# A hybrid encoder layer on one core: the dense products in seven block products instead of eight

## The chip, the cores and the metric

The kernel runs on one core of one Trainium2 chip. The core has a matrix engine (TensorE, PE in the profile; its weight loads are PEld), a vector engine (VectorE, DVE), an activation engine (ScalarE, ACT), a general engine (GpSimd, POOL) and a queue engine that starts DMA transfers (SyncE, SP). The metric is the device time of one execution in microseconds (us), and lower is better.

## The reference, cut to what matters

One layer is computed for 1024 prompt tokens and 32 sample tokens, 1056 in all, with D_MODEL = 1024 and D_FF = 2816, in float32.

```python
def swiglu(x, w_gate, w_up, w_down):
    return (jax.nn.silu(x @ w_gate) * (x @ w_up)) @ w_down

x = x + 0.5 * rmsnorm(swiglu(rmsnorm(x, ffn1_norm_pre), ffn1_w_gate, ffn1_w_up, ffn1_w_down), ffn1_norm_post)
h = rmsnorm(x, mix_norm_pre)
a, b, q, k, v, g = split(h @ w_in)                 # six blocks of 512 columns
u = a * sigmoid(b)
c = silu(layernorm(depthwise_conv31(concat(conv_hist, u))))
r = silu(g) * groupnorm(retention(rope(q), rope(k), v, R0)) * ret_gn_g   # 4 heads of 128
x = x + rmsnorm(concat([c, r]) @ w_out, mix_norm_post)
x = x + 0.5 * rmsnorm(swiglu(rmsnorm(x, ffn2_norm_pre), ffn2_w_gate, ffn2_w_up, ffn2_w_down), ffn2_norm_post)
```

The results are the new x of all tokens, the last 30 rows of u and the retention states.

## The kernel before, in words

Everything is held transposed: 128 channels on the partitions, tokens along the free dimension. The 1056 tokens are cut into three chunks `CH` of 416, 384 and 256 columns. A weight matrix is used in blocks of 128 x 128, 1312 of them in the whole layer. To keep float32 accuracy each operand is split into a high part (rounded to the matrix engine's fp32r format by an ACT copy) and a low part (the difference, a subtraction), and each product is three matmuls: high x high, high x low, low x high. That is `gemm`, lines 155 to 157.

`weight` loads 128 x 1024 weights into `raw`, writes `whi` on ACT (line 137) and `wlo` on GpSimd (line 138). `split_x` makes `xh` and `xl` of the tokens, with the norm's gain but without the norm's factor; that factor, `rbc`, is multiplied onto the result later, so the products need not wait for it.

`ffn` goes through eight groups of two or three blocks of 128 FFN channels. In each it makes gate and up products for the three chunks (`glu_unit`, tiles `pg` and `pu`; DVE lines 309, 313 and 317, ACT lines 311 and 316), splits the gated value in SBUF, and multiplies it at once by the down weights, so that gated values never leave the chip. The down products `pd` are added to `y` in SBUF by DVE (line 335). `mixer` makes the GLU and the convolution's 31 taps (DVE, lines 413 and 416, over all tokens at once, 1086 columns), the heads' q, k, v and g, and the retention in pieces of up to 128 tokens (`retain`). Between mixer and `out_proj` the results stay in SBUF too. Norms (`norm`, `pre_norm`, `post_norm`) sum squares (ACT line 229, DVE line 233), turn them into a factor and spread it over the partitions by a matmul.

The order of the work is set by two things. Small pieces that follow a product are put on a list (`later`) and emitted after a given stretch of matrix time. The framework's scheduler then places each instruction in its engine's queue, and each engine runs its queue in that order. DMAs are all started by SP.

Of the kernel before, what the change touches and what calls it, by code (L numbers as in the profile page):

```python
# [10 lines left out]
F32 = mybir.dt.float32  # L11
F32R = mybir.dt.float32r
# [7 lines left out]
NF = FF // P  # L20
TS = 32
# [3 lines left out]
CH = [(0, 416), (416, 384), (800, 256)]  # L25
RCH = [[(0, TS), (32, P), (160, P), (288, P)], [(0, P), (128, P), (256, P)], [(0, P), (128, P)]]
GAP = 30
LCH = [(0, 446), (446, 384), (830, 256)]
LGR = [[(0, P), (128, P), (256, P), (384, 62)], RCH[1], RCH[2]]
# [4 lines left out]
GAMMA = [1.0 - 2.0 ** (-5 - h) for h in range(H)]  # L34

# [8 lines left out]
# Depths of the rotating buffers, and delays between dependent pieces of work in us of TensorE time.  # L44
TMP_BUFS = 4
SS_BUFS = 4
RET_BUFS = 2
TBUFS = {"t": TMP_BUFS, "ss": SS_BUFS, "sq": 2, "sg": 2, "dg": 1}
TAP_STEP = 0.9
RET_DELAY = (4.0, 10.0, 5.0, 3.5)  # L50
NORM_DELAY = (3.0, 2.5)
TILE_DELAY = 0.004
DOWN_DELAY = 4.0
DOWN_DELAY_END = 3.0
RET_DELAY_LAST = (2.5, 5.0, 2.0, 3.0)
CNORM_STEP = 11.0
CNORM_DELAY = (46.0, 5.0, 7.0, 5.0)
OUT_UNITS = 2
GROUPS = [[0, 1], [2, 3, 4], [5, 6, 7], [8, 9, 10], [11, 12, 13], [14, 15, 16], [17, 18, 19], [20, 21]]
# [3 lines left out]
def layer_kernel(ctx: ExitStack, tc: tile.TileContext, a: dict, o: dict):  # L63
# [4 lines left out]
    wsp = ctx.enter_context(tc.tile_pool(name="wsp", bufs=6))  # L68
    raw = ctx.enter_context(tc.tile_pool(name="raw", bufs=2))
    yp = ctx.enter_context(tc.tile_pool(name="yp", bufs=1))  # L70
    act = ctx.enter_context(tc.tile_pool(name="act", bufs=17))
    tmp = ctx.enter_context(tc.tile_pool(name="tmp", bufs=2))
    sml = ctx.enter_context(tc.tile_pool(name="sml", bufs=2))
    psm = ctx.enter_context(tc.tile_pool(name="psm", bufs=4, space=PS))
# [5 lines left out]
    idh = cst.tile([P, P], F32, name="idh")  # L80
    one = cst.tile([P, P], F32, name="one")
    mhalf = cst.tile([P, 4], F32, name="mhalf")
    on512 = cst.tile([P, P], F32, name="on512")
    rcol = [cst.tile([P, 4], F32, name=f"rcol{c}") for c in range(len(CH))]
    rsq = [cst.tile([P, 4], F32, name=f"rsq{c}") for c in range(len(CH))]
    rbc = [cst.tile([P, n], F32, name=f"rbc{c}") for c, (_, n) in enumerate(CH)]
# [7 lines left out]
    # Work that follows a matrix product is emitted a given stretch of TensorE time later, between other products.  # L94
# [11 lines left out]

    def step():
        t, _, fn = heapq.heappop(pend)
        now[0] = max(now[0], t)
        fn()  # L110
# [5 lines left out]
    ready = [False] * len(CH)  # L116
    waiting = [[] for _ in CH]

    def scaled(c, fn):
        if ready[c]:  # L120
            fn()
        else:
            waiting[c].append(fn)

# [3 lines left out]
    def weight(src, eng=None, pieces=1):  # L128
        r = raw.tile([P, KD, P], F32, name=nm("raw"), tag="raw")
        hi = wsp.tile([P, KD, P], F32R, name=nm("whi"), tag="wh")  # L130
        lo = wsp.tile([P, KD, P], F32R, name=nm("wlo"), tag="wl")
        s, m = src.rearrange("p (k c) -> p k c", k=KD), KD // pieces

        def piece(i):
            e = slice(i * m, (i + 1) * m)
            nc.sync.dma_start(out=r[:, e], in_=s[:, e])
            nc.scalar.activation(hi[:, e], r[:, e], AF.Copy)  # L137
            (eng or nc.gpsimd).tensor_tensor(lo[:, e], r[:, e], hi[:, e], ALU.subtract)  # L138

        if pieces > 1:  # L140
            return (hi, lo), piece
        piece(0)
        return hi, lo

    def xtile(c, dt, s):
        return act.tile([P, CH[c][1]], dt, name=nm(s), tag=f"x{c}")

    def ttile(n, s, tag="t"):
        return tmp.tile([P, LCH[0][1]], F32, name=nm(s), tag=tag, bufs=TBUFS[tag])[:, :n]

    def gemm(ps, wx, start=True, stop=True):
        last = len(wx) - 1
        n = ps.shape[1]
        for i, ((wh, wl), (xh, xl)) in enumerate(wx):
            nc.tensor.matmul(ps, wh, xh, start=start and i == 0, stop=False)  # L155
            nc.tensor.matmul(ps, wh, xl, start=False, stop=False)  # L156
            nc.tensor.matmul(ps, wl, xh, start=False, stop=stop and i == last)  # L157
            advance(3 * (n / 2400 + 0.0025))

    def ytile(c, k, s):  # L160
        return yp.tile([P, CH[c][1]], F32, name=nm(s), tag=f"y{c}_{k}")

    def proj(c, w, xn, s):
        while len(xn[c]) < KD or None in xn[c]:
            step()
        p = mmt(CH[c][1], s)
        gemm(p, [((w[0][:, k], w[1][:, k]), xn[c][k]) for k in range(KD)])
        return p

    def mmt(n, s):  # L170
        return psm.tile([P, 512], F32, name=nm(s), tag="mm")[:, :n]

    def stt(n, s, tag="st"):
        return pss.tile([P, 512], F32, name=nm(s), tag=tag)[:, :n]

    def norm(ss, n, groups, inv, ident, done, rpre=None, rout=None, dt=(1.0, 2.5)):
        def first():
            m = len(groups)
            sp = stt(4, "sp")
# [530 lines left out]
```

## Time and profile before

| | |
|---|---|
| median of 3 runs | 2104.08 us (2102.23 to 2105.53) |
| span of the profiled execution | 2102.2 us |
| busy: PE, PEld | 2017.4 us (96%), 1980.6 us (94%) |
| busy: DVE, ACT, POOL | 995.9 us (47%), 535.9 us (25%), 641.9 us (31%) |
| matmuls recorded | 12384 |
| DMA | 124.65 MB, 59 GB/s in the mean |

The page gives the span of the profiled execution, which is its own time as far as it is known; the three timed runs lie between the span and 3.3 us above it. Rows of instruction groups read: line, engine, operation, output and inputs by the program's names, shapes and count, then the time busy, the mean of one in ns, and the engine's idle time just before them with what ended it. Rows of a stretch read: start and end, its length, then busy time and number of instructions for PE, PEld, DVE, ACT and POOL, the granted clock of the matrix engine, the busy share of the DMA engines, and GB/s. Rows in order of time read: start, duration, engine, line, operation.

### The profile page before, as it was taken

To read this page: it belongs to the slowest core of one execution; us is meant where nothing else is said; L and a number is where in the kernel's file an instruction comes from. 1 tells how busy PE (TensorE), PEld (TensorE's weight loads), DVE (VectorE), ACT (ScalarE), POOL (GpSimd) and SP (SyncE) were. 2 spreads that over 40 slices of the span, in tenths; PEclk is the share of its full clock that TensorE was granted. 3 is DMA by queue.
4 is the path that set the end of the run, shared out by engine and by line. 5 is a ranking of instruction groups with operands and counts; after the bars stand their busy time and mean duration, and the time that the engine had idled before them with its cause. 6 is when DMAs were issued, how large, how long until landed. Compare 5 with 4: busy or idle time off the path is not lost. (4 is left out here: it accounts for less than half of the span.)

```text
span 2102.2 us, 29594 instructions
## 1 busy us (share of the span) xinstructions
PE 2017.4 (96%) x12384; PEld 1980.6 (94%) x12384; DVE 995.9 (47%) x1623; ACT 535.9 (25%) x987; POOL 641.9 (31%) x386
## 2 busy tenths in 40 slices
PE   8999999999999998988989998999999999999996
PEld 7999999999999997887888997899999999999996
DVE  7123232323232378899998629513232323232336
ACT  6321212121202144223324635331111111111121
POOL 2212212121212135456546427411212121212114
PEclk9999999999999999999999999899999999999998
DMA  5111111111111232111101135211111111111113
GB/s 178 60 41 51 41 51 41 51 41 51 41 51 43 70 113 88 60 41 43 35 16 46 57 105 166 87 41 41 51 41 51 41 51 41 51 41 51 41 39 126
DMA packets 54133, 124.65 MB, mean 59 GB/s; under 512 B 7536, under 2 KB 31728, under 8 KB 54000
## 3 DMA queue, kind: packets, MB, share of 16 engines
q1 hardware_dynamic: 54000, 122.76, 17.8%
q8 instruction: 97, 1.59, 0.3%
q14 instruction: 36, 0.29, 0.0%
HBM read 109.12 MB, written 13.62 MB: 58 GB/s over the span
## 5 line engine op out<-in xcount | busy, mean ns | idle before, releaser
L138 POOL TENSOR_TENSOR wlo<-raw,whi 128x1024 fp32r<-128x1024 f32 (+1 forms) x171 | 421.4, 2469 | 1146.2 <-ACT whi L137 1142.5
L156 PE MATMUL pg<-xl,whi 128*128 128x256 f32 (+2 forms) x1152 | 375.5, 326 | 10.6 <-DVE xl L240 10.5
L155 PE MATMUL pg<-xh,whi 128*128 128x256 f32 (+2 forms) x1152 | 378.3, 329 | 7.2 <-ACT xh L239 6.4
L157 PE MATMUL pg<-xh,wlo 128*128 128x256 f32 (+2 forms) x1152 | 374.4, 325 | 0.7 <-DVE wlo L138 0.7
L155 PE MATMUL pd<-hh,whi 128*128 128x256 f32 (+2 forms) x1056 | 341.9, 325 | 5.2 <-DVE y L335 5.0
L156 PE MATMUL pu<-xl,whi 128*128 128x256 f32 (+2 forms) x1056 | 343.9, 326 | 0.0
L155 PE MATMUL pu<-xh,whi 128*128 128x256 f32 (+2 forms) x1056 | 343.5, 325 | 0.0
L157 PE MATMUL pu<-xh,wlo 128*128 128x256 f32 (+2 forms) x1056 | 342.4, 324 | 0.0
L156 PE MATMUL pd<-hl,whi 128*128 128x256 f32 (+2 forms) x1056 | 342.3, 324 | 0.0
L157 PE MATMUL pd<-hh,wlo 128*128 128x256 f32 (+2 forms) x1056 | 341.2, 323 | 0.0
L137 ACT ACTIVATE whi<-raw 128x1024 fp32r<-128x1024 f32 (+1 forms) x174 | 180.7, 1047 | 589.2 <-PE pd L156 391.6
L335 DVE TENSOR_TENSOR y<-y,pd 128x416 f32<-128x416 f32 (+2 forms) x336 | 172.7, 519 | 238.9 <-PE pd L157 238.6
L313 DVE TENSOR_TENSOR h<-sg,pu 128x416 f32<-128x416 f32 (+2 forms) x132 | 68.7, 521 | 397.2 <-PE pu L157 396.2
L156 PEld LDWEIGHTS pg<-xl,whi 128*128 128x128 f32 x1152 | 218.8, 190 | 13.4 <-DVE xl L240 12.2
L155 PEld LDWEIGHTS pg<-xh,whi 128*128 128x128 f32 x1152 | 219.1, 190 | 9.3 <-ACT xh L239 6.4
L157 PEld LDWEIGHTS pg<-xh,wlo 128*128 128x128 f32 x1152 | 219.2, 190 | 1.5 <-DVE wlo L138 0.9
L155 PEld LDWEIGHTS pd<-hh,whi 128*128 128x128 f32 x1056 | 200.8, 190 | 6.9 <-DVE y L335 5.6
L157 PEld LDWEIGHTS pd<-hh,wlo 128*128 128x128 f32 x1056 | 201.2, 191 | 1.0
L155 PEld LDWEIGHTS pu<-xh,whi 128*128 128x128 f32 x1056 | 200.6, 190 | 1.1
L156 PEld LDWEIGHTS pd<-hl,whi 128*128 128x128 f32 x1056 | 201.1, 190 | 0.5
L157 PEld LDWEIGHTS pu<-xh,wlo 128*128 128x128 f32 x1056 | 200.7, 190 | 0.8
L156 PEld LDWEIGHTS pu<-xl,whi 128*128 128x128 f32 x1056 | 200.7, 190 | 0.4
(154 smaller groups left out, 2683.8 us busy)
## 6 DMA issues: line engine op xcount, KB each, us to landing
raw<-in_wgu SPq DMA_DIRECT2D x86, 512.0 KB, 3.5
raw<-in_wd SPq DMA_DIRECT2D x44, 512.0 KB, 3.5
raw<-in_wo SPq DMA_DIRECT2D x16, 512.0 KB, 3.4
x<-x SPq DMA_DIRECT2D x32, 208.0 KB, 3.1
x<-x SPq DMA_DIRECT2D x32, 192.0 KB, 2.7
x<-x SPq DMA_DIRECT2D x32, 128.0 KB, 2.1
x<-in_x SPq DMA_DIRECT2D x16, 208.0 KB, 4.1
x<-in_x SPq DMA_DIRECT2D x16, 192.0 KB, 4.0
```

The source lines that it names most:

```text
L137: nc.scalar.activation(hi[:, e], r[:, e], AF.Copy)
L138: (eng or nc.gpsimd).tensor_tensor(lo[:, e], r[:, e], hi[:, e], ALU.subtract)
L155: nc.tensor.matmul(ps, wh, xh, start=start and i == 0, stop=False)
L156: nc.tensor.matmul(ps, wh, xl, start=False, stop=False)
L157: nc.tensor.matmul(ps, wl, xh, start=False, stop=stop and i == last)
L313: nc.vector.tensor_tensor(h32, sg, pu, ALU.mult)
L335: nc.vector.tensor_tensor(ys[c][k], ys[c][k], pd, ALU.add)
```

## The change

All dense products (gate, up, down, w_in, w_out) are done by the scheme of Strassen in Winograd's form. Two blocks of input channels, two blocks of output columns and two quarters of 264 tokens make a 2 x 2 product of blocks; it takes seven block products of sums instead of eight of blocks. The tokens are now two halves j of 528 columns, each two quarters of Q = 264.

- Weights: the host hands over the four blocks of each 2 x 2 apart. `prep` loads them into four `raw` tiles, makes four sums on DVE (lines 158, 159, 164, 167) and splits all seven into `whi` (ACT, line 151) and `wlo` (GpSimd, or DVE for two of them, line 152). Its steps run between the products of the visit before.
- Tokens: `tbuild` makes the seven token operands of a pair of channel blocks: four sums of 264 columns, two high parts on ACT, two low parts (three together as `tal`, four together as `tbl`).
- Products: `visit` runs seven products of `nk` pairs of channel blocks into three PSUM tiles `px` (two buffers), `pz` and `py` (one each). Several products go into the same bank one after the other, and each bank is read in between: eight reads, four of them copies on ACT (line 211) and four additions on DVE (line 214), or eight additions on DVE where the result is summed over blocks (line 209).
- The norm's factor is applied to the tokens before the splits (`pre_norm`), so the products wait for the norm.
- The gated values go to DRAM (`hd`); the down products run after all gate and up products, in four blocks `DBLK` of 3, 3, 3 and 2 pairs, each of which loads `hd` through two buffers (`gtile`) and builds its token operands.
- The convolution's taps run by halves, the convolution's and the heads' outputs go through DRAM (`cd`, `rd`), retention takes five pieces in each half instead of nine in all, and the rotary products move wholly to GpSimd.
- `load` and `held` tie a DMA's place in the order to the last matmul emitted.

```diff
+    def prep(src, nk, dve_lo=()):
+            a11, a21, a22, a12 = (wp.tile([P, 4 * P], F32, name=nm("raw"), tag="raw", bufs=5)[:, :nk * P] for _ in range(4))
...
+            def split(x):
+                nc.scalar.activation(hi, x, AF.Copy)
+                (nc.vector if len(ws) in dve_lo else nc.gpsimd).tensor_tensor(lo, x, hi, ALU.subtract)
...
+            split(a11)
+            nc.vector.tensor_tensor(s1, a21, a22, ALU.add)
+            nc.vector.tensor_tensor(a21, a11, a21, ALU.subtract)
+            split(s1)
+            split(a12)
+            nc.vector.tensor_tensor(a11, s1, a11, ALU.subtract)
+            split(a11)
+            nc.vector.tensor_tensor(a12, a12, a11, ALU.subtract)
+            split(a12)
+            split(a22)
+            split(a21)
...
+    def tbuild(f, dst, j, kp, pool_lo=False):
+        v.tensor_tensor(f[:, 1], f[:, 7], f[:, 0], ALU.subtract)
+        nc.scalar.activation(tah, f[:, 0:3], AF.Copy)
+        v.tensor_tensor(tal, f[:, 0:3], tah, ALU.subtract)
+        v.tensor_tensor(f[:, 3], f[:, 4], f[:, 1], ALU.subtract)
+        v.tensor_tensor(f[:, 6], f[:, 4], f[:, 7], ALU.subtract)
+        v.tensor_tensor(f[:, 5], f[:, 2], f[:, 3], ALU.subtract)
+        nc.scalar.activation(tbh, f[:, 3:7], AF.Copy)
+        (nc.gpsimd if pool_lo else v).tensor_tensor(tbl, f[:, 3:7], tbh, ALU.subtract)
...
+    def visit(ws, tj, nk, dst, acc, after, between):
+        x = bank("px", 2)
+        product(0, x, True)
+        first(dst[0], x)
+        z = bank("pz", 1)
+        product(1, z, True)
+        first(dst[3], z)
+        y = bank("py", 1)
+        product(2, y, True)
+        add(dst[0], y)
+        product(3, x, False)
+        first(dst[1], x)
+        product(4, z, False)
+        add(dst[1], z)
+        y = bank("py", 1)
+        product(5, y, True)
+        first(dst[2], y)
+        product(6, x, False)
+        add(dst[3], x)
+        add(dst[2], x)
...
+            def build(j, ht=ht, k0=k0, nk=nk):
+                for k in range(nk):
+                    f = gtile("hf")
+                    for i, to in enumerate(pieces(f)):
+                        load(to, two(hd[2 * (k0 + k) + i, :, half(j)]))
+                    tbuild(f, ht, j, k, k % 2 == 1)
```

A unit of weights serves both halves (two visits) or, at the edges of a stage where the halves come one after the other, one half (one visit); in the second case the weights are loaded and prepared again for the other half.

Where it moves instructions, three places. First, VectorE in the down products, before: the end of a group's gated values (tg, h, hl) and then nothing but the additions of products to y.

```order
L309 TENSOR_TENSOR tg_3209<-pg_3159,rbc_97 128x384
L313 TENSOR_TENSOR h_525_3213<-sg_3211,pu_3184 128x384
L317 TENSOR_TENSOR hl_3216<-h_525_3213,hh_3215 128x384
L309 TENSOR_TENSOR tg_3269<-pg_3219,rbc_98 128x256
L313 TENSOR_TENSOR h_532_3273<-sg_3271,pu_3244 128x256
L317 TENSOR_TENSOR hl_3276<-h_532_3273,hh_3275 128x256
L335 TENSOR_TENSOR y_778<-y_778,pd_3297 128x416
L335 TENSOR_TENSOR y_787<-y_787,pd_3308 128x416
```

After, in the second down block: additions from the banks (ys from px, pz, py) stand between the sums of the next token operands (hf), their low parts and the weight sums (raw, s).

```order
L209 TENSOR_TENSOR ys_5731<-ys_5731,py_6732 128x264
L214 TENSOR_TENSOR ys_5731<-ys_5731,px_6679 128x264 x2
L186 TENSOR_TENSOR hf_6664<-hf_6664 128x264
L189 TENSOR_TENSOR hf_6664<-hf_6664 128x264
L190 TENSOR_TENSOR hf_6664<-hf_6664 128x264
L191 TENSOR_TENSOR hf_6664<-hf_6664 128x264
L188 TENSOR_TENSOR tal_6668<-hf_6664,tah_6667 128x792
L193 TENSOR_TENSOR tbl_6670<-hf_6664,tbh_6669 128x1056
L209 TENSOR_TENSOR ys_5733<-ys_5733,px_6754 128x264
L209 TENSOR_TENSOR ys_5733<-ys_5733,pz_6777 128x264
L214 TENSOR_TENSOR ys_5733<-ys_5733,py_6795 128x264
L164 TENSOR_TENSOR raw_6764<-s_936_6787,raw_6764 128x384
```

Additions on which a single PSUM bank waits now have token and weight sums ahead of them on the same engine. Second, VectorE in the mixer, before: taps (cv) of one column block alternate with reads of products (q, k, g).

```order
L413 TENSOR_SCALAR cv_7867<-u_6928,vec 128x1086
L416 SCALAR_TENSOR_TENSOR cv_7867<-u_6928,vec,cv_7867 128x1086
L573 TENSOR_TENSOR q_8059<-pq_8030,cos_6912 128x416
L416 SCALAR_TENSOR_TENSOR cv_7867<-u_6928,vec,cv_7867 128x1086 x2
L573 TENSOR_TENSOR k_8095<-pk_8066,cos_6912 128x416
L416 SCALAR_TENSOR_TENSOR cv_7867<-u_6928,vec,cv_7867 128x1086 x5
L579 TENSOR_TENSOR g_8162<-pg_8133,rbc_96 128x416
```

After, early in the mixer: a tap of half the length (cu), then token sums of the second half (xf), a weight sum (raw), a weight's low part (wlo) and reads of products (cu from py, pz, px).

```order
L214 TENSOR_TENSOR cu_9947<-cu_9947,py_9998 128x264
L158 TENSOR_TENSOR s_1592_9990<-raw_9963,raw_9964 128x512
L485 SCALAR_TENSOR_TENSOR cu_9328<-cu_9328,vec 128x558
L189 TENSOR_TENSOR xf_9588<-xf_9588 128x264
L189 TENSOR_TENSOR xf_9603<-xf_9603 128x264
L188 TENSOR_TENSOR tal_9592<-xf_9588,tah_9591 128x792
L214 TENSOR_TENSOR cu_9947<-cu_9947,pz_9975 128x264
L188 TENSOR_TENSOR tal_9607<-xf_9603,tah_9606 128x792
L159 TENSOR_TENSOR raw_9963<-raw_9962,raw_9963 128x512
L214 TENSOR_TENSOR cu_9947<-cu_9947,px_9948 128x264
L152 TENSOR_TENSOR wlo_9994<-s_1592_9990,whi_9993 128x512
L485 SCALAR_TENSOR_TENSOR cu_9328<-cu_9328,vec 128x558
```

The taps keep their number of elements and stand among work that was not there. Third, the queue of SP at the start, before: weights first, then half of the last chunk of x.

```order
L612 DMA vec<-in_vec 128x196
L136 DMA raw_105<-in_wgu 128x512
L136 DMA raw_108<-in_wgu 128x512
L260 DMA x_117<-in_x 128x256
L260 DMA x_119<-in_x 128x256
```

After: both halves of x, then the first weights.

```order
L704 DMA vec<-in_vec 128x196
L712 DMA x_88<-in_x 128x528 x4
L712 DMA x_93<-in_x 128x528 x4
L715 DMA idn<-in_idn 128x128
L716 DMA msk<-in_msk 128x128
L712 DMA x_123<-in_x 128x528 x4
L712 DMA x_128<-in_x 128x528 x4
L146 DMA raw_160<-in_wgu 128x512
```

Sixteen transfers of x now stand ahead of the first weights.

More of the change, by code (lines that the diff above doesn't have):

```diff
@@ new lines, in layer_kernel, with unit, run @@
+    program = []
+    def unit(src, nk, visits, dve_lo=()):
+        program.append((src, nk, visits, dve_lo))
+    def run():
+        made = [prep(s, nk, dl) for s, nk, _, dl in program]
+        for _ in made[0][1]:
+            pass
+        for n, (src, nk, visits, _) in enumerate(program):
+            ws = made[n][0]
+            nxt = made[n + 1][1] if n + 1 < len(program) else iter(())
+            for i, (before, tj, dst, acc, after) in enumerate(visits):
+                if before:
+                    before()
+                last = i == len(visits) - 1
+                visit(ws, tj, nk, dst(), acc, after, (lambda: next(nxt, None)) if last else lambda: None)
+            made[n] = None
@@ new lines, in post_norm, with done @@
+    def post_norm(j, ys, ss, res, g, mul, out, gpre, dst):
+        def done(rb):
+            s2 = None
+            for q in range(2):
+                xs = gtile("xs")
+                for k in range(4):
+                    load(flat(xs[:, 2 * k:2 * k + 2]), res[4 * q + k, :, half(j)])
+                for k in range(4):
+                    y = ys[4 * q + k]
+                    nc.vector.scalar_tensor_tensor(y, y, col(g, 4 * q + k), rb, ALU.mult, ALU.mult)
+                    (nc.vector if gpre is None and k % 2 else nc.gpsimd).tensor_tensor(y, y, xs[:, 2 * k:2 * k + 2], ALU.add)
+                    nc.sync.dma_start(out=out[4 * q + k, :, half(j)], in_=flat(y))
+                    if gpre is not None:
+                        s2 = square(s2, y)
+            if gpre is not None:
+                pre_norm(j, ys, s2, gpre, dst)
+        norm(ss, 1.0 / D, mul, done)
@@ new lines, in layer_kernel, with then @@
+    hu(1, (0, 1))
+    cu(2, (0, 1))
+    cu(3, (0, 1))
+    for j in (0, 1):
+        hu(2, (j,), True)
+        hu(3, (j,), True)
+        src, nk, vs, dl = program[-1]
+        b, tj, dst, acc, after = vs[0]
+        def then(after=after, j=j):
+            after()
+            free(j)
+        program[-1] = (src, nk, [(b, tj, dst, acc, then)], dl)
+    out_proj(xt[2], x1, "mpost", x2, "f2pre", xt[3])
+    ffn(xt[3], a["wgu2"], a["wd2"], x2, "f2post", o["y"], None, None, 2)
+    run()
+    flush()
```

848 lines of the change are left out of this document (397 added, 451 removed).

## The prediction

> **What bounds the kernel now.** I read the page's busy shares first, then busy time by stage, then the start times of consecutive matmuls, then pairs of VectorE and GpSimd instructions that run at the same time, and last the groups by form for prices.
>
> ```profile
> span 2102.2 us, 29594 instructions
> PE 2017.4 (96%) x12384; PEld 1980.6 (94%) x12384; DVE 995.9 (47%) x1623; ACT 535.9 (25%) x987; POOL 641.9 (31%) x386
> ```
>
> TensorE is the bound over the whole; no other engine is half busy. The average hides one stage. The next rows are stretches of the span (us from its start), with busy time of PE, PEld, DVE, ACT and POOL: first the FFN, then the mixer, then the output product, then the second FFN.
>
> ```profile
> 65.00:784.00 719.00, 716.93 (x4432) 713.27 (x4431) 234.87 (x374) 141.63 (x228) 153.15 (x69) 1.00 0.16 52
> 784.00:1184.00 400.00, 357.62 (x2195) 336.95 (x2194) 368.95 (x584) 139.74 (x308) 223.00 (x167) 0.97 0.15 48
> 1184.00:1284.00 100.00, 99.39 (x624) 98.03 (x623) 44.30 (x77) 42.87 (x82) 43.55 (x27) 1.00 0.36 116
> 1290.00:2060.00 770.00, 757.95 (x4638) 751.26 (x4637) 269.05 (x440) 160.18 (x269) 179.68 (x91) 0.99 0.16 53
> ```
>
> In the FFNs PE never stops and DVE has two thirds of its time free. In the mixer DVE is busy 369 of 400 us, more than PE. So a cheaper matmul pays in the FFNs and hardly in the mixer, and added VectorE work costs at once in the mixer.
>
> **What a matmul costs.** These are starts of matmuls in a full stretch; between them lie 36 matmuls of 416 columns, 48 of 384 and 48 of 256.
>
> ```profile
> 299.82 0.35 PE L155 MATMUL pg<-xh,whi 128*128 128x416 f32 x1
> 306.62 0.34 PE L155 MATMUL pg<-xh,whi 128*128 128x384 f32 x1
> 315.07 0.28 PE L155 MATMUL pg<-xh,whi 128*128 128x256 f32 x1
> 320.82 0.35 PE L155 MATMUL pg<-xh,whi 128*128 128x416 f32 x1
> ```
>
> Start to start is 0.1889, 0.1760 and 0.1198 us. Before, each of 3936 weight passes (1312 blocks by three) runs over the three chunks: 3936 x 0.4847 = 1908 us of the 2102. After, the order holds 13,776 matmuls of 264 columns. Eight columns above 256, at the slope between 256 and 384 (0.00044 us a column), give 0.1233 us, so 1699 us: TensorE's products lose 209 us, 11%, not an eighth, because the narrower matmul pays its fixed part more often. [...]
>
> **What VectorE and GpSimd cost each other.** Here are four instructions of the FFN (DVE, POOL, DVE, POOL) and six of the mixer.
>
> ```profile
> 322.35 2.42 DVE L317 TENSOR_TENSOR hl<-h,hh 128x256 fp32r<-128x256 f32 x1 [0.83 <-ACT hh L316]
> 322.09 2.40 POOL L138 TENSOR_TENSOR wlo<-raw,whi 128x1024 fp32r<-128x1024 f32 x1 [0.48 <-ACT whi L137]
> 344.36 0.42 DVE L313 TENSOR_TENSOR h<-sg,pu 128x256 f32<-128x256 f32 x1 [2.52 <-PE pu L157]
> 342.48 2.40 POOL L138 TENSOR_TENSOR wlo<-raw,whi 128x1024 fp32r<-128x1024 f32 x1 [17.99 <-ACT whi L137]
> ...
> 1002.34 0.15 DVE L501 SCALAR_TENSOR_TENSOR nb<-mv,rs 128x1 f32<-128x1 f32 x1
> ...
> 1012.75 1.34 DVE L416 SCALAR_TENSOR_TENSOR cv<-u,vec,cv 128x1086 f32<-128x1086 f32 x1
> 1014.00 0.55 DVE L573 TENSOR_TENSOR q<-pq,cos 128x384 f32<-128x384 f32 x1
> 1014.47 1.64 DVE L416 SCALAR_TENSOR_TENSOR cv<-u,vec,cv 128x1086 f32<-128x1086 f32 x1
> 1013.27 1.69 POOL L574 TENSOR_TENSOR sw<-sw,sin 128x384 f32<-128x384 f32 x1 [2.15 <-ACT sw L572]
> 1015.04 1.96 POOL L575 TENSOR_TENSOR q<-q,sw 128x384 f32<-128x384 f32 x1
> ```
>
> The 256-column subtraction of two SBUF tensors took 2.42 us and ended 0.28 us after the GpSimd instruction beside it; 256 columns at 0.96 a ns are 0.27 us. It stood still until GpSimd was through. The product that reads PSUM took 0.42 us in the same situation. In the mixer taps and GpSimd take turns: the tap at 1012.75 ends at 14.09, GpSimd's product ends at 14.96, the next tap at 16.11, GpSimd's sum at 17.00. [...]
>
> **Prices.**
>
> ```profile
> L138 POOL TENSOR_TENSOR wlo<-raw,whi 128x1024 fp32r<-128x1024 f32 (+1 forms) x171 | 421.4, 2469 | 1146.2 <-ACT whi L137 1142.5
> L335 DVE TENSOR_TENSOR y<-y,pd 128x416 f32<-128x416 f32 (+2 forms) x336 | 172.7, 519 | 238.9 <-PE pd L157 238.6
> L335 DVE TENSOR_TENSOR y<-y,pd 128x256 f32<-128x256 f32 x112 | 46.5, 420 | 63.8 <-PE pd L157 63.8
> L317 DVE TENSOR_TENSOR hl<-h,hh 128x416 fp32r<-128x416 f32 x44 | 26.1, 592 | 25.5 <-ACT hh L316 25.3
> L138 DVE TENSOR_TENSOR wlo<-raw,whi 128x1024 fp32r<-128x1024 f32 x1 | 1.2, 1221 | 0.0
> L416 DVE SCALAR_TENSOR_TENSOR cv<-u,vec,cv 128x1086 f32<-128x1086 f32 x120 | 193.2, 1610 | 0.9
> L501 DVE SCALAR_TENSOR_TENSOR nb<-mv,rs 128x1 f32<-128x1 f32 x28 | 29.5, 1055 | 4.6 <-POOL rs L498 4.6
> L138 POOL TENSOR_TENSOR wlo<-raw,whi 128x512 fp32r<-128x512 f32 x2 | 2.6, 1316 | 7.3 <-ACT whi L137 7.3
> L442 POOL TENSOR_TENSOR sin<-sin,rbc 128x256 f32<-128x256 f32 x1 | 0.7, 735 | 0.0
> L137 ACT ACTIVATE whi<-raw 128x1024 fp32r<-128x1024 f32 x170 | 178.3, 1057 | 586.5 <-PE pd L156 391.6 <-PE pg L156 65.5 <-issue 54.5
> L333 ACT ACTIVATE y<-pd 128x256 f32<-128x256 f32 x16 | 6.1, 382 | 4.5 <-PE pd L157 4.5
> ```
>
> DVE: 0.157 us plus columns/960 (592 at 416, 1221 at 1024). Queued instructions start some 0.08 us before the one ahead has ended (the tap at 1012.75 ends at 1014.09, its successor starts at 1014.00), so I count 0.08 less each. GpSimd: 0.735 at 256 and 2.40 at 1024 give 0.18 us plus 2.17 ns a column: 1.01 at 384, 1.29 at 512, 2.47 at 1056.
>
> **The change, part by part.** *PSUM evictions.* Each visit of a pair of weight columns by a token half reads its banks eight times. 928 adds on DVE at 0.35 us are 325 us, for 336 adds of 173 us before; the other 544 copies go to ACT at 0.39 (382 at 256), 212 us. *Weight sums.* 472 new DVE additions (0.61, 0.48 and 0.34 us at 512, 384 and 256 columns), 258 us. *Low halves of weights.* Seven where four were: GpSimd 474 x 1.29 + 168 x 1.01 + 80 x 0.74 = 840 us against 421 before; 104 more on DVE, 55 us. *Token sums (tbuild).* 408 DVE instructions, 207 us, in place of the splits of x and h; 48 large ones on GpSimd, 119 us. *Taps.* 248 half-length ones, 159 us alone, where 120 take 161 us alone (1.34 each). *Gated values, norms, squares:* 290 instructions of 528 columns, 183 us. Retention (40 chunks for 36), diagonals and small pieces: 90 us. DVE sums to 1270 us, GpSimd (with rotary, residual sums and GLU) to 1130 where it was busy 642. ACT comes to about 1050 us, nowhere above two thirds of a stage, so I cost it at nothing. DRAM: the gated values are stored and read again, some 56 MB more on 123; the queues stood at 52 GB/s in the FFN rows above and have carried 327 at the start (row below), so only latency counts.
>
> By stage, from the order of the new kernel. **Gate and up** (each FFN): TensorE 3696 x 0.1233 = 456 us, DVE 172 to 194, GpSimd some 230. TensorE stays the bound; 911 us for both, where they took 352 blocks x 3 x 0.4847 = 512 each. Gain 113. **Down**: TensorE 1848 x 0.1233 = 228 us. DVE 219 us in FFN 1 and 199 in FFN 2, GpSimd about 150, now in the same stretch. How much of GpSimd's time does DVE lose? Above nothing, at most all. The mixer before is the nearest: taps lost 120 x (1.61 - 1.34) = 32 us, the one-column nb 28 x (1.055 - 0.15) = 25, smaller groups about 24 by the same subtraction: 81 us, against some 177 that GpSimd's work there needs alone, 0.46. So DVE takes 219 + 69 = 288 and 268 us, 560 for both (256 each before, TensorE's price). Cost 48. **Mixer and output product**: DVE 355 + 96 = 451 us, GpSimd 340, so 451 + 0.46 x 340 = 607; DVE was 92% busy in the mixer before, I take 95% and 640 us, where it took 500. Cost 140. TensorE has 331 us of products there and some 80 of retention and norms (357.6 less 192 x 3 x 0.4847 before). What hid such work before, TensorE's own time, is gone there.
>
> **Edges.**
>
> ```profile
> 7.00:20.00 13.00, 11.12 (x60) 9.63 (x59) 12.19 (x23) 12.57 (x28) 5.56 (x3) 1.00 0.95 327
> 6.40 0.58 PE L155 MATMUL pg<-xh,whi 128*128 128x256 f32 x1 [6.40 <-ACT xh L239]
> 2088.45 0.42 DVE L233 TENSOR_TENSOR ss<-ss,sq 128x256 f32<-128x256 f32 x1 [0.21 <-ACT sq L229]
> x<-x SPq DMA_DIRECT2D x32, 208.0 KB, 3.1
> ```
>
> *Start.* TensorE began at 6.4 us because the norm's factor was applied after the product. Now all of x (4.3 MB, 14 us at 327 GB/s) is queued ahead of the first weights, the norm must be done before the first token sum, and its PSUM copies stand on ACT behind 16 squares and 7 weight splits: first product near 28 us, a stream near 40, so 35 us are lost. *Each of eight down blocks* loads its hd tiles through two buffers; the third tile waits for a build and a 3.1 us load: 2.5 us each beyond DVE's sum, 20 us. *FFN 2's first single visits* run beside the norm of the second half: 15 us. *Tail*: from the last square (2088.5) to the end were 14 us; with 528 columns 20.
>
> Sum: 35 + 911 + 560 + 640 + 20 + 15 + 20 = 2201 us against the span of 2102.2 (1024 + 512 + 500, and 66 of edges). The median of the runs, 2104.08, lies 2 us above the span, so 2203.
>
> **Rivals.** [...] (c) *Everything serial*: DVE plus GpSimd, 219 + 150, 199 + 150 and 791, gives 35 + 911 + 718 + 791 + 55 = 2510; against it stands the 0.46.
>
> **How the numbers follow.** My forecast has 0.60, (a) 0.25, (b) with its neighbourhood 0.14, (c) 0.01. Differences under 0.2% cannot be told from none. (b) I split 0.06 faster, 0.04 same, 0.04 slower. That makes faster 0.31, same 0.04, slower 0.65. The forecast's own range is 2120 to 2300 (DVE's loss between 0.33 and 0.6 of GpSimd's time). To leave out no more than two in ten the range goes down to 1980, into (a), where DVE would lose a tenth: 1980 to 2300.
>
> **What would show it.** Matmuls of 264 columns 0.123 us apart in gate and up; down stages near 290 us with DVE over 90% busy; wlo of 512 columns well over 1.29 us and DVE's raw sums well over 0.69 in the mean, in turns as above; mixer and output near 640 us with PE about 60% busy; first product near 28 us. I am wrong if PE stays above 90% busy outside the gate and up stretches, if DVE's two-input means stay near 0.157 us plus columns/960, or if gate and up are not at TensorE's pace because an eviction on ACT or DVE comes too late for the single banks of z and y.

## The result, and the profile after

The changed kernel takes 2529.49 us in the median of four runs (2521.77 to 2531.05), the kernel before beside it 2103.15: a ratio of 1.2017, 95% interval 1.1998 to 1.2036. Slower was right; 2203 us was 326 too few, and the time lies outside the range of 1980 to 2300. The profiled execution has a span of 2527.7 us, so its parts are set against the 2201 us of the sum. One of the four runs of e10 below took 2611.72 us at a granted clock of 0.716, where its other three had 0.895 to 0.898; the ratio is that of the three.

From the page after: the span, the busy times, and the tenths of PE and of the granted clock in 40 slices.

```profile
span 2527.7 us, 38826 instructions
PE 1995.7 (79%) x14440; PEld 1918.9 (76%) x14440; DVE 1708.7 (68%) x2842; ACT 983.8 (39%) x1932; POOL 1315.2 (52%) x946
PE   3799999978978545577757676766999999789874
PEclk8899999989988867779878877777999999889986
```

TensorE is busy 79% where it was 96%, and no other engine is full either. Now by stage: three pieces of the start, then gate and up, down, mixer, output product, gate and up of FFN 2, down of FFN 2 with the end. Columns: length, busy time with count of PE, PEld, DVE, ACT and POOL, granted clock, DMA share, GB/s. A stage begins here where ScalarE first copies one of its products out of PSUM.

```profile
0.00:41.50 41.50, 7.91 (x32) 5.94 (x32) 25.82 (x46) 17.85 (x30) 11.20 (x11) 1.00 0.49 167
41.50:130.00 88.50, 61.54 (x402) 58.64 (x403) 76.85 (x93) 39.86 (x68) 55.30 (x30) 0.83 0.18 60
130.00:500.00 370.00, 370.00 (x3041) 369.92 (x3041) 142.44 (x252) 150.23 (x308) 180.05 (x126) 1.00 0.24 78
60.00:547.00 487.00, 460.41 (x3685) 457.12 (x3685) 227.79 (x366) 202.43 (x403) 246.25 (x168) 0.97 0.25 80
547.00:918.00 371.00, 284.56 (x1911) 270.08 (x1910) 269.07 (x509) 133.22 (x249) 172.09 (x144) 0.82 0.26 80
918.00:1487.00 569.00, 376.56 (x2477) 349.95 (x2475) 526.81 (x815) 217.00 (x454) 352.09 (x241) 0.81 0.21 65
1487.00:1658.00 171.00, 115.82 (x745) 108.00 (x745) 132.08 (x204) 76.51 (x143) 101.38 (x63) 0.77 0.26 87
1658.00:2179.00 521.00, 471.48 (x3705) 464.31 (x3706) 265.82 (x411) 213.49 (x429) 274.34 (x184) 0.95 0.27 88
2179.00:2527.00 348.00, 270.12 (x1857) 255.88 (x1855) 245.24 (x474) 116.15 (x223) 149.28 (x134) 0.85 0.28 88
```

In the full stretch 3041 matmuls take 370 us, 0.1217 each: the price of a matmul was right (0.1233). All that was lost lies outside such stretches. At 0.1217 the 14,440 matmuls (the small ones of norms and retention counted alike) need 1757 us; 770 us are stops and slow matmuls. In the two down stages every engine has free time: VectorE is busy 73 and 70%, TensorE 77 and 78%.

What TensorE waited for, longest in total first (us, times, longest):

```profile
PE px L221 <- ACT tah L187: 115.5, 31, 18.4
PE sp L279 <- DVE ss L307: 62.4, 7, 15.7
PE px L221 <- DVE tal L188: 54.5, 36, 3.0
PE bc L292 <- DVE dg L287: 26.1, 9, 7.3
```

All four are token operands (tah, tal) and norms (ss, dg), together 258.5 of the 532 us in which TensorE stands. That looks less like a rate of work than like a chain that begins too late; the experiments test it.

### The profile page after: what moved, and what is told of

Same layout as the page of the kernel before. It is cut to its first block, busy times and chain, and to the rows that moved or that the text cites. A ratio compares the mean times of both kernels' runs of the same rounds, so it can differ in the third digit from the quotient of the medians.

```text
span 2527.7 us, 38826 instructions
## 1 busy us (share of the span) xinstructions
PE 1995.7 (79%) x14440; PEld 1918.9 (76%) x14440; DVE 1708.7 (68%) x2842; ACT 983.8 (39%) x1932; POOL 1315.2 (52%) x946
## 5 line engine op out<-in xcount | busy, mean ns | idle before, releaser
L152 POOL TENSOR_TENSOR wlo<-raw,whi 128x512 fp32r<-128x512 f32 (+2 forms) x656 | 859.6, 1323 | 805.3 <-ACT whi L151 755.7
L151 ACT ACTIVATE whi<-raw 128x512 fp32r<-128x512 f32 (+2 forms) x708 | 395.4, 576 | 498.4 <-PE px L221 183.1
L221 PE MATMUL px<-tbh,whi 128*128 128x264 f32 x1312 | 397.6, 303 | 57.4 <-ACT hd L211 22.5
L221 PE MATMUL px<-tbh,wlo 128*128 128x264 f32 x1312 | 389.0, 297 | 3.9 <-POOL wlo L152 3.7
L221 PE MATMUL px<-tbl,whi 128*128 128x264 f32 x1312 | 389.3, 297 | 1.3 <-POOL tbl L193 1.3
L221 PEld LDWEIGHTS px<-tbh,whi 128*128 128x128 f32 x1312 | 264.6, 202 | 65.0 <-ACT hd L211 23.3
L221 PE MATMUL px<-tah,whi 128*128 128x264 f32 x656 | 205.3, 313 | 122.9 <-ACT tah L187 115.5
L221 PEld LDWEIGHTS px<-tbh,wlo 128*128 128x128 f32 x1312 | 263.2, 201 | 6.1 <-POOL wlo L152 5.8
L221 PEld LDWEIGHTS px<-tbl,whi 128*128 128x128 f32 x1312 | 263.7, 201 | 1.8 <-POOL tbl L193 1.5
L485 DVE SCALAR_TENSOR_TENSOR cu<-cu,vec 128x558 f32<-128x558 f32 (+1 forms) x240 | 262.8, 1119 | 0.5
L221 PE MATMUL px<-tal,whi 128*128 128x264 f32 x656 | 206.2, 314 | 55.5 <-DVE tal L188 54.5
```

The lines of the kernel that those rows point to most:

```text
L151: nc.scalar.activation(hi, x, AF.Copy)
L152: (nc.vector if len(ws) in dve_lo else nc.gpsimd).tensor_tensor(lo, x, hi, ALU.subtract)
L221: mm = nc.tensor.matmul(ps, l[:, w], r, start=start and k == 0 and i == 0, stop=k == nk - 1 and i == 2, skip_group_check=True)
L485: nc.vector.scalar_tensor_tensor(cc, u[:, t:t + m], vec[:, w + t:w + t + 1], cc, ALU.mult, ALU.add)
```

## Experiments

Theory L: VectorE and GpSimd, taking turns, pace every stage outside gate and up, only with a larger loss than 0.46. Theory S: the loss lies at the seams, the places where the operands of the next block, half or stage are made in a chain over four engines. All results stand in one table; each ratio is against the kernel before, run in turn on the same chip, and the stages are cut as above.

| kernel | us | ratio, 95% interval | start, gate/up 1 | down 1 | mixer | output | gate/up 2 | down 2, end |
|---|---|---|---|---|---|---|---|---|
| predicted | 2203 | | 491 | 300 | 640 with output | | 471 | 300 |
| changed | 2529.5 | 1.2017 (1.1998-1.2036) | 548 | 371 | 569 | 171 | 521 | 349 |
| e1 no low halves | 2307.7 | 1.0982 (1.0965-1.0998) | 530 | 344 | 468 | 136 | 495 | 332 |
| e8 no weight sums | 2394.5 | 1.1397 (1.1376-1.1417) | 538 | 342 | 527 | 146 | 506 | 329 |
| e9 no token sums | 2325.3 | 1.1061 (1.1040-1.1082) | 521 | 302 | 542 | 149 | 507 | 302 |
| e10 no taps | 2380.0 | 1.1320 (1.1301-1.1339) | 548 | 369 | 419 | 176 | 518 | 351 |
| e2 early | 2497.0 | 1.1880 (1.1862-1.1897) | 541 | 353 | 572 | 172 | 514 | 339 |
| e13 spread | 2523.9 | 1.2009 (1.1989-1.2030) | 541 | 371 | 575 | 170 | 513 | 353 |
| e14 low halves on DVE | 2456.4 | 1.1687 (1.1670-1.1705) | 548 | 350 | 538 | 155 | 519 | 343 |
| e6 fill | 2524.5 | 1.2011 (1.1994-1.2029) | 546 | 371 | 568 | 166 | 517 | 353 |
| e4 = e1, own dg | 2278.6 | 1.0841 (1.0823-1.0860) | 519 | 345 | 467 | 135 | 487 | 327 |
| e5 = e1, five f | 2309.1 | 1.0978 (1.0957-1.1000) | 531 | 346 | 466 | 140 | 495 | 331 |
| e11 = e1, three g | 2299.4 | 1.0937 (1.0921-1.0953) | 527 | 340 | 477 | 141 | 495 | 319 |
| e3 eight late | 2267.3 | 1.0789 (1.0771-1.0807) | 547 | 308 | 451 | 141 | 515 | 302 |
| e7 = e3, two mends | 2214.3 | 1.0536 (1.0514-1.0558) | 536 | 295 | 450 | 136 | 507 | 287 |
| e12 = e7, start | 2229.0 | 1.0606 (1.0582-1.0629) | 543 | 298 | 453 | 137 | 508 | 289 |
| e15 = e7, DVE lows | 2184.7 | 1.0410 (1.0387-1.0433) | 534 | 299 | 422 | 130 | 510 | 289 |
| e16 seven, mends | 2449.4 | 1.1655 (1.1632-1.1679) | 535 | 352 | 543 | 159 | 513 | 344 |
| e17 = e15, eight all | 2221.5 | 1.0566 (1.0548-1.0584) | 563 | 299 | 425 | 117 | 530 | 288 |

### Leaving one kind of work out (e1, e8, e9, e10)

```diff
e1   -(nc.vector if len(ws) in dve_lo else nc.gpsimd).tensor_tensor(lo, x, hi, ALU.subtract)
     -ws.append((hi, lo))
     +ws.append((hi, wl0[:, :nk * P]))          # one tile of zeros
e8   -s1 = a21 + a22; a21 = a11 - a21; split(s1); ... a11 = s1 - a11; ... a12 = a12 - a11
     +split(a21)                                # and splits of the blocks as loaded
e9   -f1 = f7 - f0; f3 = f4 - f1; f6 = f4 - f7; f5 = f2 - f3     # in tbuild; splits of 7 slots
     +                                          # splits of the 4 loaded slots
e10  -if t + 1 < CW:
     +if t + 1 < 2:
```

> Left out: the low halves of all weights; every product reads one constant tile of zeros in their place, so that GpSimd loses 656 subtractions (859.6 us busy) and VectorE 52. TensorE's work is unchanged. Theory L (the prediction's: VectorE and GpSimd take turns, and their sum paces every stage outside gate and up, only with a larger loss than 0.46): outside gate and up GpSimd holds some 500 us of low halves; VectorE gets 0.46 of it back, 230 us, and its own 52 subtractions, 40 us: about 2260. Theory S (seams: the loss sits where the next token operands are late, in a chain of single steps on four engines, and in a clock that is about half for some 6.6 us behind each stop): the chain is only shortened where a wlo stands ahead of a tbl or of r, 60 to 100 us: 2430 to 2470.

> The changed kernel without the sums of weights: the seven products of a unit read splits of a11, a21, a12, a11, a12, a22, a21 as loaded; 472 VectorE additions are gone, everything else stands. They are 270 us busy at 512 columns and some 80 more at 384 and 256 in the trace, about 200 of it outside gate and up. Theory L (VectorE's and GpSimd's sum paces every stage outside gate and up): 200 us less, about 2330. Theory S (only what lies in the chains at the seams and in stretches where a unit serves one visit counts): 80 to 130 less, 2400 to 2450.

> The changed kernel without the sums of tokens: the seven products read the four split blocks of tokens as they are; five small VectorE instructions of each of 68 token blocks are gone, and the splits take four slots instead of seven. Some 140 us of VectorE for the sums, 45 for the smaller low halves, 50 of GpSimd. Theory S: these are the chains that the first products wait for (115 us of stops on tah, 54 on tal); each gets about a third shorter, and the norms' chains too: 60 to 90 less, 2440 to 2470. Theory L: 0.46 x 50 + 185: about 2320.

> The changed kernel with 2 of the 31 taps of the convolution: 232 VectorE instructions of 528 or 558 columns, 258 us busy in the trace, are gone, all between 950 and 1390 us. Theory L: the mixer is VectorE's and all of it is won: 2270. Theory S: retention's chain, the evictions behind it and the norms still set a pace there, TensorE's own 330 us too: 130 to 180 less, 2350 to 2400.

e1 takes away 722 subtractions of GpSimd's and 104 of VectorE's (656 and 52 were announced). It saves 222 us, between the theories and nearer to L; it does so in mixer and output (136) and hardly where L wanted it, in the down stages (27 and 17). e8 saves 135, nearer to S. e9 saves 204, as L said in total, but the work it takes away (there are four sums of a block, not five; 304 instructions in all) lies in the wrong place for L: 69 and 47 us in the down stages, where VectorE had a quarter of its time free. The first down stage of e9, to be set against the row of 371 us above, and its waits:

```profile
521.00:823.00 302.00, 258.21 (x1888) 246.07 (x1888) 212.46 (x406) 114.84 (x244) 157.08 (x142) 0.91 0.31 95
PE px L217 <- ACT tah L187: 34.8, 21, 5.0
PE px L217 <- DVE tal L188: 33.5, 22, 5.5
```

The stops on tah fall from 115.5 us to 34.8, those on tal from 54.5 to 33.5. So S has the place right and the size two to three times too small. VectorE does 57 us less in the first down stage (269 to 212), and though it had time free, the stage is 69 us shorter: this work was paid in full and a little more. Not all of it is sums. The 304 sums are 162 us of VectorE's time in the changed kernel; e9 also splits four slots for seven, so VectorE does 186 us less in all, ScalarE 53 and GpSimd 57. How much of the 204 us belongs to the narrower splits was not separated. e10 saves 150 us, all of it in the mixer and within S's range: 419 us are left there, of which TensorE is busy 335.

### Moving work (e2, e13, e14)

```diff
e2   # in ffn, for every down block
-    start of the block: build(0); build(1)
+    before the last visit of the stage ahead: build(0);  start of the block: build(1)
e13  +before the last visit of the stage ahead: build(0);  before the second half's first visit: build(1)
e14  -program.append((src, nk, visits, dve_lo))
     +program.append((src, nk, visits, dve_lo if gate[0] else tuple(range(7))))    # gate[0]: in gate and up
```

> The token sums of the first half of each down block are built ahead of the last visit of the stage before instead of behind it; the same instructions, in another place. Theory S: the stops before the first products of the down blocks (waits on tah and tal at 535 to 727 and 2166 to 2356 us in the trace) are 34 us in each FFN; about half of them go, and with each the slow spacing behind it: 2470 to 2490. Theory L: no work is saved and GpSimd and VectorE still take turns: 2515 to 2530.

> The changed kernel with the token blocks of a down block built in two places: those of the first half ahead of the last visit of the block before (as in the run that took 2497.0 us), those of the second half ahead of the second half's own first visit instead of the first half's. The same instructions. Theory P (place: VectorE works in order, and the evictions of the first visit stand behind the second half's sums): 10 to 25 us less than 2497 in each FFN, 2450 to 2480. Theory A (amount and chain length: the second half's first product then waits for its own chain instead): 2490 to 2515.

> The changed kernel with all low halves of weights outside gate and up on VectorE instead of GpSimd: some 390 subtractions, 474 us busy on GpSimd in the trace, become about 0.60, 0.47 and 0.34 us each on VectorE, 190 us more there (90 of it in mixer and output product). Theory T (turns: what GpSimd does there VectorE loses at about 0.44, 75 us in the mixer and 18 in the output product by the run without low halves): mixer and output product even out, the down stages have VectorE idle 27 per cent of the time: 2515 to 2550. Rival F (GpSimd's help is nearly free and only the length of its instructions delays): 90 us and more are added, 2600 to 2650. Rival G (waiting for GpSimd costs VectorE more than the work): 2430 to 2490.

Early token blocks (e2) are worth 32 us, a little less than S said; L saw nothing there. Putting the second half's sums off to its own visit (e13) loses 27 of them again: theory P is wrong, and A, which ended at 2515, is missed by 9 us too. The sums are better early even if evictions stand behind them.

e14 falls into the range of rival G, against T and F. VectorE takes over the subtractions outside gate and up, and the kernel gets 73 us faster: 30 in the mixer, 16 in the output product, 27 in the down stages, where VectorE is busy 23 and 28 us more. For the changed kernel the rows of mixer and output product stand above (569 and 171 us long). Here they are in e14, and behind them in e1, which has no low halves at all:

```profile
897.00:1436.00 539.00, 365.98 (x2481) 339.40 (x2480) 504.91 (x929) 217.40 (x456) 199.44 (x135) 0.81 0.22 70
1436.00:1591.00 155.00, 107.21 (x749) 101.72 (x747) 133.39 (x239) 77.38 (x143) 57.03 (x28) 0.80 0.29 96
```

```profile
873.00:1341.00 468.00, 347.92 (x2481) 327.56 (x2479) 419.11 (x789) 215.45 (x455) 182.52 (x135) 0.86 0.25 81
1341.00:1477.00 136.00, 104.35 (x744) 99.58 (x744) 100.06 (x187) 76.50 (x144) 39.40 (x22) 0.84 0.33 109
```

The next rows are groups of the whole kernel (mean in ns behind the busy time): taps and VectorE's own low halves of 512 columns, first in the changed kernel, then in e14.

```profile
L485 DVE SCALAR_TENSOR_TENSOR cu<-cu,vec 128x558 f32<-128x558 f32 x120 | 135.0, 1138 | 0.1
L152 DVE TENSOR_TENSOR wlo<-s,whi 128x512 fp32r<-128x512 f32 x36 | 37.8, 1050 | 1.9 <-ACT whi L151 1.8
L152 DVE TENSOR_TENSOR wlo<-raw,whi 128x512 fp32r<-128x512 f32 x36 | 37.8, 1049 | 2.8 <-ACT whi L151 2.2
```

```profile
L488 DVE SCALAR_TENSOR_TENSOR cu<-cu,vec 128x558 f32<-128x558 f32 x120 | 109.1, 920 | 0.0
L152 DVE TENSOR_TENSOR wlo<-raw,whi 128x512 fp32r<-128x512 f32 x180 | 143.8, 813 | 6.8 <-ACT whi L151 6.4
L152 DVE TENSOR_TENSOR wlo<-s,whi 128x512 fp32r<-128x512 f32 x40 | 35.0, 874 | 0.1
```

GpSimd's busy time in mixer and output product falls by 197 us (453 to 256). VectorE gets 102 us of subtractions more in these two stages (47 to 149) and is yet busy 21 less (659 to 638): it lost 123 us to those 197, 0.62. By e1 it is 140 less, 47 of them its own low halves, for 232 of GpSimd: 0.40. The turns can be seen in the changed kernel too (a tap, a weight sum and a low half on VectorE; a low half and the gated product on GpSimd):

```profile
1273.10 1.82 DVE L485 SCALAR_TENSOR_TENSOR cu<-cu,vec 128x558 f32<-128x558 f32 x1
1274.84 1.79 DVE L159 TENSOR_TENSOR raw<-raw,raw 128x512 f32<-128x512 f32 x1
1276.56 0.68 DVE L152 TENSOR_TENSOR wlo<-s,whi 128x512 fp32r<-128x512 f32 x1
1272.45 1.87 POOL L152 TENSOR_TENSOR wlo<-raw,whi 128x512 fp32r<-128x512 f32 x1 [2.54 <-ACT whi L151]
1274.28 1.80 POOL L467 TENSOR_TENSOR cu<-cu 128x528 f32<-128x528 f32 x1
```

The weight sum ends 0.55 us after GpSimd's product, though 512 columns take 0.68 when nobody is in the way, as the low half behind it shows.

### Buffers and the clock (e4, e5, e11, e6)

```diff
e4   -dg = hbuf("dg", "sq", 1)
     +dg = hbuf("dg", "dg", 1)                  # and two buffers for sq
e5   -FBUFS = 4
     +FBUFS = 5
e11  -fp.tile([P, 8, Q], F32, name=nm(s), tag="g", bufs=2)
     +fp.tile([P, 8, Q], F32, name=nm(s), tag="g", bufs=3)
e6   +for _ in range(12 if k else 24):          # in product 0 of a half's first down visit
     +    nc.tensor.matmul(d, wh[:, 0:P], wh[:, 0:256], start=True, stop=True)
```

> On top of the kernel without low halves of weights (2307.7 us): the diagonals dg of the norm get a tile of their own and the squares sq two buffers instead of one that all of them share. In the trace of the changed kernel the factor r of the first half was there at 20 us, and dg, which waits for the shared tile, was written at 32.9, behind all eight squares of the second half; a square and its sum alternated at 1.42 us. Theory S: every norm pair loses some 10 us that way, at the start, before the mixer, before FFN 2: 30 to 45 us less, 2265 to 2280. Theory L: the same VectorE and ScalarE instructions, so within 8 us of 2308.

> On top of the kernel without low halves of weights (2307.7 us): five buffers of the eight-slot tiles (x, h, ys, cu, hd) instead of four. In the mixer of the changed kernel an eviction into hd stood on ScalarE until 1289.6 us for a convolution tile whose taps were not through, and TensorE stood 15.7 us. Theory S: the mixer is held by such tiles, 15 to 35 us less, 2273 to 2293. Theory L: VectorE's work in the mixer is the same, within 8 us of 2308.

> On top of the kernel without low halves of weights (2307.7 us): three buffers of the tiles in which token blocks are loaded and summed (hf, xf, xs, cn, rf), where there were two. In that kernel's trace the six token blocks of a down block come in three rounds of some 10 us (loads issued at 596 and 607 us, each landing 3 us later, then the sums in line on VectorE), 30 us beside 15 us of TensorE's first two visits. Theory B1 (the round trip through two buffers, load behind sums, sets the pace at the block starts): about 5 us less at each of 8 block starts and a few at the norms, 2255 to 2275. Theory B2 (the sums themselves, in line on VectorE ahead of the evictions, are the pace, however early the load): within 12 us of 2308.

> The changed kernel with 768 matmuls of 256 columns that nobody reads, put where TensorE stands before the first product of each of the 16 first visits of a down block (24 ahead of the first contraction block, 12 ahead of each further one: 94 us of added TensorE work in all, by 0.12 us each). In the trace a stop of 2 us or more is followed by matmuls 0.22 us apart instead of 0.122, for 3 to 6.5 us. Theory S with the clock as its second half: the added matmuls lie in the stops and keep the spacing at 0.122, so the down stages gain 2 to 2.5 us for each of 16 visits against an overhang of at most 94 - 68 us of measured stops: 2500 to 2530, and the matmuls behind the stops stand 0.122 us apart. Theory L, with the spacing no matter because VectorE sets the pace: the overhang is added, 2530 to 2570.

The first three stand on e1, because only without low halves is there room in SBUF. e4 hits: 29 us less. The changed kernel's first norm, factor on GpSimd and diagonals on VectorE:

```profile
18.45 1.80 POOL L283 TENSOR_TENSOR r<-v,mhalf 88x6 f32<-88x6 f32 x1
31.63 0.70 DVE L307 TENSOR_TENSOR ss<-ss,sq 128x528 f32<-128x528 f32 x1
32.85 1.13 DVE L287 TENSOR_SCALAR dg<-idn,r 88x88 f32<-88x88 f32 x6
```

The factor is there at 20.3 us, its diagonals start at 32.9, once the second half's last square is summed; in e4, with a tile of their own, they start at 16.4. e5 misses: nothing is won, so the 15.7 us stop behind a convolution tile was not on the path that counts, at least without low halves (the longest of these stops is 11.6 us in e1 and 7.5 in e5). e11 wins 8 us, within B2's range: the round trip through two buffers is not the pace. The down stages do get 4 and 13 us shorter, of the 40 that B1 put there, and mixer and output product 14 longer. e6 puts 720 matmuls ahead of the first products of the down blocks (768 were announced; the last blocks have two contraction blocks, not three). At 0.12 us each they are 86 us of TensorE work, and the kernel takes 2524.5 us, the same as the changed kernel within the intervals: that much room there is. The spacing behind the stops did not become 0.122 throughout, as announced: of 552 slow matmuls in the two down stages (0.18 to 0.27 us from start to start) 384 are left. Those that went did not set the pace; on the others e6 says nothing.

### Fewer seven products (e3, e7, e12, e15, e16, e17)

```diff
e3   prep, eight:   +for x in (a11, a12, a21, a22): split(x)
     tbuild, eight: splits of the four blocks of tokens, no sums
     visit, eight:  four banks, two products of blocks each, four evictions
     used in down, mixer and output product; gate and up unchanged
e7   = e3 + early as in e2 + dg in a tile of its own (raw: four buffers for five)
e12  = e7 + second half of x loaded and normed after the first product; two pairs of single units first
e15  = e7 + low halves outside gate and up on VectorE
e16  = changed kernel + early + own dg + low halves outside gate and up on VectorE (raw: four buffers for five)
e17  = e15 with eight products in gate and up too
```

> Seven products in gate and up only; down, mixer and output product take eight products of plain blocks (no weight sums, no token sums, four evictions of a visit instead of eight, four low halves instead of seven), everything else as in the changed kernel. TensorE gets 8/7 of the work there: 84 us more over 4,800 matmuls. Theory L: VectorE and GpSimd fall to about what they were before in these stages, so down is at TensorE's price (2 x 257) and mixer with output product near 520: about 2130. Theory S: the seams stay (norms between the stages, loads at each block start, the start of the kernel), only their chains lose the sums: 2230 to 2300.

> Seven products in gate and up only (2267.3 us), and two of the seams mended: token blocks of the down stages built one visit earlier, dg in a tile of its own (for which the raw weights have four buffers instead of five). Theory S: early builds are worth 32 us in the changed kernel; with eight products their chains are shorter, 15 to 20; dg 25 to 40: 2205 to 2230. Theory L: VectorE and GpSimd have the same work: 2255 to 2270.

> On top of the kernel with seven products in gate and up only and two seams mended (2214.3 us): the second half of x is loaded, squared and normed only once the first product has been issued, and FFN 1 runs two pairs of units on single halves at its start, as FFN 2 does, instead of one. Theory S (the start is a chain in which the first half waits behind the second on three engines): first eviction at 45 us instead of 58 and fewer stops before 130 us, 10 to 25 less, 2190 to 2204. Rival: the second half's chain is only late by as much, 2210 to 2220.

> Seven products in gate and up only with early token blocks and dg in a tile of its own (2214.3 us), and the low halves of weights outside gate and up on VectorE. With seven products that move was worth 73 us; here it moves four low halves of a unit instead of five to seven, and VectorE is busy some 100 of 300 us in the down stages. Theory T (GpSimd beside VectorE costs more than the work itself): 30 to 50 less, 2165 to 2185. Rival: the mixer's VectorE has no room for 60 more subtractions, 2205 to 2230.

> Seven products everywhere with all three mends: low halves outside gate and up on VectorE (73 us alone), early token blocks (32 alone), dg in a tile of its own (29 alone, with two buffers for sq, which are not in this one; raw weights have four buffers). If they add up: 2390 to 2410. If VectorE, which took the subtractions, is now ahead of the token blocks: 2420 to 2440.

> Eight products everywhere, in the changed kernel's frame (token halves of 528 columns, gated values through DRAM, norm ahead of the product), otherwise as the kernel with seven in gate and up only (2184.7 us). TensorE gets 2 x 528 x 0.1217 = 128 us more in gate and up. If the full stretches give that gain and the fronts cost it nothing: 2300 to 2315. If the fronts of gate and up take back a part (token sums in the norm's chain; without token sums these stages were 31 us shorter, without weight sums 20): 2250 to 2285. If they take back all: 2184 or less.

e3 and e7 come out as S said. e12 misses on both sides and is 15 us slower: the first copy out of PSUM comes at 55 us instead of 58, but gate and up end 8 us later. e15 gains 30, at the edge of T's range. e16 shows that the mends do not add up: 7 us beyond e14 alone, where 46 to 66 were expected, and above the second range too (2420 to 2440). Its four raw buffers may be the reason: TensorE's stops at pz for whi are 41.1 us, and 16.2 in e14, which has five. A run with five and the other two mends was not made.

e17 falls between all the ranges announced for it (2250 and more, or 2184 and less) and closes the account. Gate and up of FFN 1 from 58 us on, seven products (e15) and eight (e17):

```profile
58.00:534.00 476.00, 460.01 (x3698) 457.56 (x3698) 216.17 (x356) 200.01 (x405) 238.27 (x161) 0.98 0.26 83
58.00:562.00 504.00, 502.16 (x4125) 501.95 (x4125) 68.89 (x65) 153.33 (x320) 118.73 (x90) 1.00 0.26 76
```

The first copy out of PSUM comes at 57.9 us in e15 and at 47.0 in e17, so with eight products this row leaves out the first 11 us. In all, seven products take 528 matmuls out of the stage, 64 us, and end it 28 us earlier. Over the kernel they are worth 37 us (2221.5 to 2184.7) of the 128 that TensorE is spared in gate and up; with eight, the output product ahead of FFN 2's norm is 13 us shorter as well. So the 428 us that lie between the changed kernel and the kernel before in these runs (2101) are, taken in this order of steps: 120 for the frame with eight products and the three mends (token halves, norm ahead of the product, gated values through DRAM), 37 won in gate and up, 265 lost by seven products in down, mixer and output (e16 less e15, both with four raw buffers), 80 by the places that the mends mend (changed less e16). The best version tried is still 4.1% above the kernel before.

## Why the prediction was wrong

*TensorE's price: right.* 0.1217 us a matmul, 450 us of products for each gate and up where 456 were counted.

*Start and fronts: 50 put, 157 measured.* Start with gate and up took 548 for 491, FFN 2's gate and up 521 for 471. The first product of the blocks starts at 41.5 us, where I put 28, and the first copy out of PSUM at 60. By 130 us 434 matmuls had run, 53 us of work: 77 lost, not 35. The step "a stream near 40" took the first product as the end of the chain. Each half must make four token blocks in line, and dg stood behind the other half's squares; without token sums the two stages are 26 and 14 us shorter, with dg's own tile 11 and 8 (against e1). "FFN 2's first single visits, 15 us" failed the same way.

*Down: 600 put with block starts and end, 720 measured.* This is the step that failed in kind. The sum 219 + 69 was not too small: VectorE is busy 269 us, under the 288. But the stage takes 371, since I let the stage last as long as its busiest engine. "Over 90% busy" was my own test, and it says no at 73%. Block starts were priced at 2.5 us by the load, and a third buffer for those loads (e11, without low halves) brings 17 us over both stages. The token sums were an item of VectorE's total, and are at the head of TensorE's chain: without them, and with narrower splits, each down stage is 302. What keeps these 302 above TensorE's 225 was not taken apart; in the first, TensorE is busy 258 us and stands 44.

*Mixer and output: 640 put, 740 measured.* In the mixer VectorE is nearly full, as predicted, and the size was wrong; the output product is again no stage that VectorE fills. VectorE is busy 659 us for 607, in the mixer 93%, in the output product only 77%, where I took 95% for both. The mis-sized terms are GpSimd's 340 us, which the trace shows as 453 (its low halves of 512 columns, priced at 1.29 us, took 1.58 in the mean of these stages and 1.25 at the least), and the 95%, which is 89% over both stages. The 0.46 holds with the busy time measured: 451 + 0.46 x 453 = 659, though the 451 was never measured alone, and leaving out (e1) or moving (e14) gives 0.40 and 0.62. e14, where these two stages are 30 and 16 us shorter, shows that the subtractions cost more beside VectorE than on it.

*Nothing for ACT:* no stage shows ScalarE over half busy, and no experiment made it the cause; a wait on tah is mostly a wait on the sums that VectorE makes ahead of it (of ScalarE's idle time before tah 92 us end with a sum, 36 with a DMA load).

*Rivals.* The chances of (a) and (b), 0.25 and 0.14, were my estimate, and no run shows either: in (a), which set the range's lower end of 1980, VectorE would lose a tenth of GpSimd's time, where e1 and e14 give 0.40 and 0.62; (b) was split around no change, and the kernel is 20% slower. (c), everything serial, 2510, is the nearest number, and its 219 + 150 = 369 us for the first down stage is nearly the 371 measured. By e1 that is luck. If the two engines' work were the length of the stage, 129 us less on GpSimd would have shortened it by as much; it is 27 us shorter, and 344 us long with VectorE and GpSimd busy 236 and 43:

```profile
529.60:873.40 343.80, 268.40 (x1905) 256.79 (x1904) 235.91 (x485) 133.30 (x247) 43.44 (x21) 0.86 0.27 83
```

The wrong half of the forecast is that it stands on totals, and (c) too. The trace of before, with TensorE 96% busy, had 17 stops of over 1.5 us to price one by, the longest 7.7 us at the start of FFN 2; the changed kernel has 106, up to 18.4.

## What to carry to other kernels

Price work at its place: here an instruction ahead of a block's first product was paid in full and a little more, and work in the middle of a full stretch was nearly free (e8 takes 74 us of VectorE's work out of the first gate and up, which gets 9 us shorter). Where no engine is nearly full in a stage (in the down stages here none was over 78% busy), look for a chain: see what the bounding engine waits for, and take that out once before counting loads. Cutting an eighth of the products won 37 us here in gate and up and lost 265 in the other stages, so ask where the sums that replace them will stand. And half of a shared load moved to a slower engine may cost more than doing it oneself: 73 us here (e14), with 512 columns at 1.25 us on GpSimd and 0.66 on VectorE at the least.

## What the hardware showed

The trace of the changed kernel has 24 stops of TensorE of 2 us or more with 20 product matmuls straight behind them; behind 23 of these stops at least 12 of the 20 start 0.18 to 0.27 us apart, and that lasts 3.0 to 7.4 us (e1's expectation has 6.6 behind each). Starts behind one of them; of the rows left out, all but three follow each other by the same 0.22:

```profile
640.55 0.28 PE L221 MATMUL py<-tal,whi 128*128 128x264 f32 x1
640.67 0.28 PE L221 MATMUL py<-tah,wlo 128*128 128x264 f32 x1
643.78 0.59 PE L221 MATMUL px<-tah,whi 128*128 128x264 f32 x1 [2.83 <-ACT tah L187]
644.16 0.42 PE L221 MATMUL pz<-tah,whi 128*128 128x264 f32 x1
644.38 0.42 PE L221 MATMUL py<-tah,whi 128*128 128x264 f32 x1
...
649.81 0.42 PE L221 MATMUL px<-tah,whi 128*128 128x264 f32 x1
650.03 0.38 PE L221 MATMUL px<-tal,whi 128*128 128x264 f32 x1
650.25 0.29 PE L221 MATMUL px<-tah,wlo 128*128 128x264 f32 x1
650.38 0.28 PE L221 MATMUL pz<-tbh,whi 128*128 128x264 f32 x1
```

The spacing is 0.12 us, after a stop of 2.83 us it is 0.22 for 6.3 us, at a granted clock of 0.50, then 0.12 again at 0.98. About 1300 product matmuls of the trace stand 0.18 to 0.27 us before the next, 128 us more than at 0.1217; the forecast counted none of it. In e6 the down stages with their stops filled are 371 and 353 us long, not shorter than 371 and 349, so the third of the slow spacing that went there was a sign of the stops and not what they cost; what the rest costs, and what it costs in the mixer, was not tried.

GpSimd beside VectorE can be dearer than VectorE alone: 73 us less with the same subtractions on VectorE (e14), which was the busier of the two.
